# Output projection by token blocks instead of by column halves, with two token blocks routed early and the other two apart

## The chip, the cores and the metric

The kernel runs on one core of a Trainium2 chip. The metric is the device time of one launch in microseconds; the median of three runs is given. The engines are named as the profile names them: PE is TensorE (matmuls; PEld its weight loads), DVE is VectorE, ACT is ScalarE, POOL is GpSimd, SP issues the DMA transfers.

## The reference, cut to what matters

One encoder layer over 512 tokens of 1024 channels: three mixers, merged by gates, one output projection, layer norm, then a mixture of 16 experts in which each expert picks its 64 tokens by router affinity, and a second layer norm. The change lies between the merged mixers and the first expert:

```python
x = layer_norm(DN_ALPHA * x + merged @ w_out[l], ln_mix_g[l], ln_mix_b[l])
...
aff = jax.nn.softmax(jnp.einsum('bsd,de->bse', x, router_w).astype(jnp.float32), axis=-1)
gate, idx = lax.top_k(jnp.swapaxes(aff, 1, 2), cap)
xs = jax.vmap(lambda xb, ib: xb[ib])(x, idx)
h = jax.nn.silu(jnp.einsum('becd,edf->becf', xs, w_gate)) * jnp.einsum('becd,edf->becf', xs, w_up)
y = jnp.einsum('becf,efd->becd', h, w_down) * gate[..., None].astype(x.dtype)
```

## The kernel before

The order of instructions on each engine is the order of the code (a manual schedule); engines run ahead of each other until a tile isn't ready. Tokens lie in four blocks of 128 (tb 0 to 3), the 1024 output columns of the projection in two halves of 512.

**Projection.** Each fp32 product is made of three fp32r matmuls (`wo_mm`, L805 to L807): high part of the merged activations (mh) by high weights (woh), mh by low weights (wol), low activations (ml) by woh. The weights arrive raw (wor) and are split into woh and wol by ScalarE and VectorE (`split`, L88 and L89), one slice of 128 rows (k) at a time. Half 0 runs with k outside and the four blocks inside (L1017 to L1023), into four PSUM banks pw0 to pw3; half 1 runs block by block (`pass2`), with the routing of earlier blocks between its pieces.

**Routing.** `resid` (L931, L932) adds the projection to alpha times x (in the tile xres) and takes statistics of the row half. `route_t` (L954) transposes a block's half to channels first on TensorE, ScalarE copies it to x1T (L955, in the tile hbt). `route_m` (L962) multiplies by the router weights gW (tile Sg) into the bank prt: four fp32 matmuls, the tokens as the stationary operand, 16 moving columns. As layer norm isn't applied yet, the logits are put right afterwards: `aggr` and `stats` give mean and inverse deviation of a row (rss; L936, L942, L502 to L509), `centered` (L981) subtracts the mean's share, `soft` and `soft2` are the softmax (L988 to L996; the exponential on ScalarE, L991), `route_a` (L1002, L1004) transposes the affinities to affT, 16 experts on partitions. `top64` searches the 64 largest of a stretch of tokens, eight at a time (L1011, L1013): sA over tokens 0 to 255 (blocks 0 and 1), sB over tokens 256 to 511. Behind sB come a threshold, ranks, one-hot matrices (L1146), then `gather` (L1163) and the experts. `rows` (L976, L977) scales the tokens on ScalarE for the gather.

**Weights of the experts.** Each 2 MB quarter of a gate, up or down matrix (e0g, e0u, e0d, e1g, ...) goes to one of ten buffers, which it shares with woh, wol, mh and ml of the projection; SP issues the transfers in program order (L79), and one that waits for its buffer holds those behind it. e0g takes buffers free early; two quarters of e0u follow when woh and wol of half 0 are done with; the other two and two of e0d when woh, wol of half 1 and mh, ml are; the first quarter of e1g when the first quarter of e0g has been multiplied (`ff_mm`, L1215).

Of the kernel before, what the change touches and what calls it, by code (L numbers as in the profile page):

```python
# [10 lines left out]
OP = mybir.AluOpType  # L11
# [17 lines left out]
def tile_hybrid_layer(ctx, tc, pk, w2p, xT, x, wlv, wa, wak, wmb, wout, eg, eu, ed, gb, out):  # L29
    nc = tc.nc  # L30
    V, A, G, PE, SP = nc.vector, nc.scalar, nc.gpsimd, nc.tensor, nc.sync
# [37 lines left out]
    def P(name):  # L69
        return psum.tile([128, 512], F32, name=name, tag="ps")  # L70
# [4 lines left out]
    def C(name, shape, dt=F32):  # L75
        return cpool.tile(shape, dt, name=name)
# [51 lines left out]
    ident = C("ident", [128, 128])  # L128
# [158 lines left out]
    st = {}  # L287
# [211 lines left out]
    def rsqrt(r, h, t):  # L499


        return [lambda: V.tensor_scalar(t.bitcast(I32), h.bitcast(I32), 1, None, op0=OP.logical_shift_right),  # L502
                lambda: V.tensor_scalar(r.bitcast(I32), t.bitcast(I32), -1.0,
                                        float(0x5f3759df - 2 ** 22 - 2 ** 31), op0=OP.mult, op1=OP.add),
                lambda: V.tensor_mul(t, r, r), lambda: V.tensor_mul(t, t, h),
                lambda: V.scalar_tensor_tensor(r, t, -1.5, r, op0=OP.add, op1=OP.mult),
                lambda: V.tensor_mul(t, r, r), lambda: V.tensor_mul(t, t, h),
                lambda: V.scalar_tensor_tensor(t, t, -5.0 / 3.0, t, op0=OP.add, op1=OP.mult),
                lambda: V.scalar_tensor_tensor(r, t, 1.25, r, op0=OP.add, op1=OP.mult)]  # L509

    def weave(a, b):

        for i in range(max(len(a), len(b))):
            run(a[i:i + 1] + b[i:i + 1])

    def run(fs):
        for f in fs:
            f()
# [207 lines left out]
    for n, nm in enumerate(names):  # L726
# [4 lines left out]
        for g in range(nseg[n]):  # L731
            k0, k1 = (8 * g + nseg[n] - 1) // nseg[n], (8 * g + 8 + nseg[n] - 1) // nseg[n]
# [44 lines left out]
    def xr_(tb):  # L777
        return xres[tb // 2][:, tb % 2, :]
# [16 lines left out]
    def wo_split(half, k):  # L795
        c = k // 4
        if (half, 0) not in woh:
            wo_tiles(half)
        return split(wraw[half, c][:, k % 4, :], woh[half, c][:, k % 4, :], wol[half, c][:, k % 4, :])

    def wo_mm(p, half, k, tb):
        c, kk = k // 4, k % 4
        a = mh[c][:, kk, tb * 128:(tb + 1) * 128]
        b = ml[c][:, kk, tb * 128:(tb + 1) * 128]
        PE.matmul(p, a, woh[half, c][:, kk, :], start=k == 0, stop=False)  # L805
        PE.matmul(p, a, wol[half, c][:, kk, :], start=False, stop=False)
        PE.matmul(p, b, woh[half, c][:, kk, :], start=False, stop=k == 7)  # L807
# [37 lines left out]
    for u in range(24):  # L845
        b, j = order[u // 8], u % 8
# [45 lines left out]
    def X(name, shape, dt=F32):  # L892
        return xp.tile(shape, dt, name=name)
# [3 lines left out]
    x1T = hbt.rearrange("p (a b c) -> p a b c", a=4, b=4)  # L897
    xga = X("xga", [128, 1024])
# [9 lines left out]
    rb, gW = (sgf[:, 128 * i:128 * i + 128].rearrange("p (k e) -> p k e", k=8) for i in range(2))  # L908
# [6 lines left out]
    mvs = small[:, 0:8].rearrange("p (a b) -> p a b", a=4)  # L915
    rss, nrs, nmr, rts, mnl, zs = (small[:, 8 + 4 * i:12 + 4 * i] for i in range(6))
# [12 lines left out]
    def resid(tb, half, p):  # L929
        r = xr_(tb)[:, half * 512:(half + 1) * 512]  # L930
        V.scalar_tensor_tensor(r, r, ALPHA, p, op0=OP.mult, op1=OP.add)  # L931
        V.bn_stats(stat[:, tb, half, :], r)  # L932

    def aggr(tb, n):

        return [lambda i=i: V.bn_aggr(mvs[:, i, :], stat[:, i]) for i in range(tb, tb + n)]  # L936

    def stats(tb, n):

        c = slice(tb, tb + n)  # L940
        v = mvs[:, c, 1]
        ops = [lambda: V.tensor_scalar(v, v, H225, H225 * 1e-5, op0=OP.mult, op1=OP.add)]  # L942
        return ops + rsqrt(rss[:, c], v, rts[:, c])

    def every2(d):

        c = d // 2 * 256 + d % 2
        return slice(c, c + 255, 2)

    def route_t(tb, half):  # L950

        p = P("px")
        for k in range(4):
            PE.transpose(p[:, k * 128:(k + 1) * 128], xr_(tb)[:, every2(half * 4 + k)], ident)  # L954
        A.copy(x1T[:, tb], p.rearrange("p (a b) -> p a b", a=4))  # L955

    def route_m(tb, half):

        if not half:
            prt[tb] = P("prt")  # L960
        for k in range(4):
            PE.matmul(prt[tb][:, 0:16], x1T[:, tb, k, :], gW[:, 4 * half + k, :], start=half == k == 0,  # L962
                      stop=half == 1 and k == 3)

    prt = {}
# [6 lines left out]

    def rows(tb):

        r = xr_(tb)
        G.tensor_mul(nmr[:, tb:tb + 1], mvs[:, tb, 0:1], nrs[:, tb:tb + 1])  # L976
        A.activation(r, r, AF.Identity, scale=rss[:, tb:tb + 1], bias=nmr[:, tb:tb + 1])  # L977

    def centered(tb, n):

        return [lambda i=i: V.scalar_tensor_tensor(aff[:, i, :], sW, mvs[:, i, 0:1], prt[i][:, 0:16], op0=OP.mult,  # L981
                                                   op1=OP.subtract) for i in range(tb, tb + n)]

    def soft(tb, n):

        for i in range(tb, tb + n):
            lg = aff[:, i, :]
            V.scalar_tensor_tensor(lg, lg, rss[:, i:i + 1], bW, op0=OP.mult, op1=OP.subtract)  # L988
        V.tensor_reduce(mnl[:, tb:tb + n], aff[:, tb:tb + n, :], axis=AX.X, op=OP.min)
        for i in range(tb, tb + n):  # L990
            A.activation(aff[:, i, :], aff[:, i, :], AF.Exp, scale=-1.0, bias=mnl[:, i:i + 1],  # L991
                         accum_out=zs[:, i:i + 1])

    def soft2(tb, n):
        V.reciprocal(zs[:, tb:tb + n], zs[:, tb:tb + n])
        V.tensor_mul(aff[:, tb:tb + n, :], aff[:, tb:tb + n, :],  # L996
                     zs[:, tb:tb + n, None].to_broadcast([128, n, 16]))

    def route_a(tb, n, beside=()):
        p = P("pat")  # L1000
        for i in range(n):
            PE.transpose(p[:16, i * 128:(i + 1) * 128], aff[:, tb + i, :], ident)  # L1002
        run(beside)
        V.tensor_copy(affT[:, tb * 128:(tb + n) * 128], p[:16, :n * 128])  # L1004
# [8 lines left out]
                ops.append(lambda t=t: V.match_replace(src, t, src, -1.0))  # L1013
        return ops

    pw = [P(f"pw{tb}") for tb in range(4)]
    for k in range(8):  # L1017
        if k + 2 < 8:
            wo_split(0, k + 2)
        if k >= 2:  # L1020
            wo_split(1, k - 2)
        for tb in range(4):
            wo_mm(pw[tb], 0, k, tb)  # L1023
    wo_split(1, 6)
    wo_split(1, 7)

# [1 line left out]
    load_halves(3, [S("e0d30", [128, 2048]), spare.tile([128, 2048], F32, name="e0d31")])  # L1028
    load_pairs(NPAIR)

    pw2 = {}

    def pass2(tb, k0=0, k1=8):
        if k0 == 0:
            pw2[tb] = P("pw2")
        for k in range(k0, k1):
            wo_mm(pw2[tb], 1, k, tb)

    L, R = slice(0, 512), slice(512, 1024)
    G.tensor_mul(gW, pkt[:, PK_RW:PK_RW + 128].rearrange("p (a b) -> p a b", a=8),  # L1040
                 pkt[:, PK_G1:PK_G1 + 8, None].to_broadcast([128, 8, 16]))
    G.tensor_mul(rb, pkt[:, PK_RW:PK_RW + 128].rearrange("p (a b) -> p a b", a=8),
                 pkt[:, PK_B1:PK_B1 + 8, None].to_broadcast([128, 8, 16]))
    A.activation(zs[:, 0:1], one[:, 0:1], AF.Exp)
    for tb in range(4):
        resid(tb, 0, pw[tb])
    for i, t in enumerate((rb, gW)):
        V.tensor_reduce(rsum[:, i, :], t.rearrange("p k e -> p e k"), axis=AX.X, op=OP.add)
    pass2(0)
    pbw = P("pbw")  # L1050
    PE.matmul(pbw[:, 0:32], ones, rsum.rearrange("p a b -> p (a b)"), start=True, stop=True)
    V.tensor_copy(bsW, pbw[:, 0:32].rearrange("p (a b) -> p a b", a=2))
    for tb in range(4):
        route_t(tb, 0)
    resid(0, 1, pw2[0])
    pass2(1, 0, 4)
    for tb in range(2):
        route_m(tb, 0)
        pass2(1, 4 + 2 * tb, 6 + 2 * tb)
    route_t(0, 1)  # L1060
    resid(1, 1, pw2[1])
    pass2(2, 0, 2)
    route_t(1, 1)
    route_m(0, 1)
    pass2(2, 2, 4)
    route_m(1, 1)
    run(aggr(0, 2) + stats(0, 2) + centered(0, 2))
    soft(0, 2)
    soft2(0, 2)
    pass2(3, 0, 3)  # L1070
    route_a(0, 2)
    pass2(3, 3, 4)
    pass2(2, 4, 8)
    sA = top64(topA, affT[:, 0:256])
    run(sA[:6])
    resid(2, 1, pw2[2])
    pass2(3, 4, 8)
    route_m(2, 0)
    route_t(2, 1)
    route_m(3, 0)  # L1080
    run(sA[6:9])
    resid(3, 1, pw2[3])
    route_t(3, 1)
    route_m(2, 1)
    route_m(3, 1)
    run(aggr(2, 2))
    s23 = stats(2, 2)
    weave(s23[:8], sA[9:12])
    weave(s23[8:], centered(2, 2))
    soft(2, 2)  # L1090
    run(sA[12:13])
    soft2(2, 2)
    route_a(2, 2, sA[13:])
    G.tensor_scalar(nrs, rss, -1.0, None, op0=OP.mult)
    for tb in range(4):
        rows(tb)

    def bcast(i, half, dg, scale=1.0, E=V, after=None):

# [34 lines left out]
    for tb in range(4):  # L1134
        PE.matmul(rk[:, :, 1, :], onesb, mk[:, tb:tb + 1, 0, :].to_broadcast([128, 4, 16]), start=False,
                  stop=tb == 3)
# [53 lines left out]
    def acc_(tb):  # L1190
        return acc[tb // 2][:, tb % 2, :]
# [260 lines left out]
    for h, c in enumerate((L, R)):  # L1452
        A.activation(acc_(3)[:, c], pf[3, h], AF.Copy, scale=rss[:, 3:4])
        for tb in range(3):
            r = acc_(tb)[:, c]
# [71 lines left out]
```

## Time and profile before

| | |
|---|---|
| median of 3 runs | 1437.47 us (1436.44 to 1439.5) |
| the profiled execution | 1437.92 us |
| its span, first to last instruction | 1436.2 us |
| PE busy | 1358.9 us (95%) |
| DVE busy | 419.3 us (29%) |
| ACT busy | 292.0 us (20%) |
| HBM read | 446.10 MB |

The span and the device time of the profiled execution differ by 1.7 us, which lie outside of the span. PE's busy share is high in all stages, as the ends of pipelined matmuls are modelled; it doesn't tell whether a stage waits for weights. That is read from the DMA share by stretches and from what SP's queue waits for. Times within the trace count from the first instruction.

### The profile page before, as it was taken

The page shows a single profiled execution, that of the slowest core. Times are in us where ns is not written, and L with a number is a line of the kernel's source. Part 1 is how long each engine was busy: PE and PEld are TensorE (multiplying, and loading weights), DVE is VectorE, ACT ScalarE, POOL GpSimd, SP SyncE. Part 2 cuts the span into 40 slices and gives each one's busy share as a digit, 9 for nine tenths or more (in the row PEclk, how much of TensorE's full clock was granted, in tenths as well). Part 3 has the DMA queues.
Part 4 walks back from the last instruction along what each step waited for, and adds up shares of the span by engine and source line. Part 5 has one row for each costly group of instructions (what it writes and reads, how often), then busy time and mean ns, then how long its engine had stood idle before and what let it go on. Part 6 is the DMA issues. An engine that isn't in the chain of part 4 may idle for free.

```text
span 1436.2 us, 17310 instructions
## 1 busy us (share of the span) xinstructions
PE 1358.9 (95%) x7425; PEld 768.3 (53%) x7425; DVE 419.3 (29%) x878; ACT 292.0 (20%) x554; POOL 24.2 (2%) x49
## 2 busy tenths in 40 slices
PE   9999999999999899999999999988989898898996
PEld 8877777888888753443443443433333343333433
DVE  5593975323445613112011011002001011100315
ACT  4644544222233210110110110110000110011110
POOL 0010000000000000000000000000000000000000
PEclk9999999999999999999999999999999999999998
DMA  6120122223239789999999999999999999999994
GB/s 231 45 90 30 61 75 72 88 93 105 89 126 406 297 327 410 429 427 428 428 426 429 427 428 428 426 428 429 426 427 429 427 429 428 428 428 428 426 403 160
DMA packets 45452, 449.31 MB, mean 313 GB/s; under 512 B 4312, under 2 KB 8536, under 8 KB 19520
## 3 DMA queue, kind: packets, MB, share of 16 engines
q1 hardware_dynamic: 45376, 448.22, 75.6%
q8 instruction: 58, 0.95, 0.3%
q14 instruction: 18, 0.15, 0.0%
HBM read 446.10 MB, written 2.10 MB: 312 GB/s over the span
## 4 chain that ended last, share of the span: by engine, by line
PE 55%; DMA 39%; DVE 3%; SPq 1%; ACT 1%; issue 0%; DVEq 0%; POOL 0%; ACTq 0%
PE py L1224 6%; PE pgt L1215 6%; PE pup L1215 5%; PE pa L266 3%; PE pm L866 3%; PE pm L867 3%; PE pm L868 3%; DMA e13d<-in_ed_dram 3%; DMA e9d<-in_ed_dram 3%; DMA e6u<-in_eu_dram 3%; DMA e10u<-in_eu_dram 3%; PE pa L268 3%; PE pa L267 3%; DMA e12u<-in_eu_dram 3%; DMA e8u<-in_eu_dram 3%; DMA e14u<-in_eu_dram 3%
## 5 line engine op out<-in xcount | busy, mean ns | idle before, releaser
L1208 DVE TENSOR_TENSOR acc<-acc,pcb 128x512 f32<-128x512 f32 x64 | 41.1, 683 | 215.5 <-PE pcb L1206 215.5
L1383 DVE TENSOR_TENSOR hbt<-pup,hbt 128x512 f32<-128x512 f32 (+1 forms) x34 | 22.3, 660 | 279.7 <-PE pup L1215 279.6
L1163 PEld LDWEIGHTS pxg<-Sg,xres 128*128 128x128 f32 x512 | 65.2, 196 | 51.5 <-issue 46.8
L266 PE MATMUL pa<-xh,wb 128*128 128x512 f32 x200 | 82.8, 414 | 0.0
L1163 PE MATMUL pxg<-Sg,xres 128*128 128x128 f32 x512 | 76.2, 292 | 6.5 <-DVE Sg L1146 6.5
L268 PE MATMUL pa<-xh,wb 128*128 128x512 f32 x200 | 78.3, 391 | 0.0
L267 PE MATMUL pa<-xl,wb 128*128 128x512 f32 x200 | 78.2, 391 | 0.0
L866 PE MATMUL pm<-xh,wm 128*128 128x512 f32 x192 | 74.8, 390 | 0.0
L867 PE MATMUL pm<-xl,wm 128*128 128x512 f32 x192 | 74.7, 389 | 0.0
L868 PE MATMUL pm<-xh,wm 128*128 128x512 f32 x192 | 74.7, 389 | 0.0
L1233 DVE SCALAR_TENSOR_TENSOR yl<-py,small,late 64x512 fp32r<-64x512 f32 x30 | 22.5, 750 | 140.9 <-ACT late L1232 140.9
L1232 ACT ACTIVATE late<-py,small 64x512 fp32r<-64x512 f32 x30 | 20.5, 683 | 195.2 <-PE py L1224 183.1
L1165 ACT ACTIVATE xgb<-pxg,pk 128x128 f32<-128x128 f32 x32 | 14.7, 458 | 157.0 <-PE pxg L1163 157.0
L1397 ACT COPY hbt<-pht 128x512 f32<-128x512 f32 (+1 forms) x18 | 9.8, 551 | 168.9 <-PE pht L1396 168.4
L1165 ACT ACTIVATE xga<-pxg,pk 128x128 f32<-128x128 f32 x32 | 14.7, 458 | 142.5 <-PE pxg L1163 142.5
L266 PEld LDWEIGHTS pa<-xh,wb 128*128 128x128 f32 x200 | 37.5, 187 | 11.2 <-issue 2.9
L226 DVE TENSOR_TENSOR wm<-wr,wm 128x1536 fp32r<-128x1536 f32 x24 | 42.0, 1752 | 4.1 <-ACT wm L223 4.1
L1372 ACT ACTIVATE hbt<-pgt 128x512 f32<-128x512 f32 x32 | 19.0, 597 | 116.7 <-PE pgt L1215 116.7
L268 PEld LDWEIGHTS pa<-xh,wb 128*128 128x128 f32 x200 | 37.5, 188 | 8.4
L267 PEld LDWEIGHTS pa<-xl,wb 128*128 128x128 f32 x200 | 37.6, 188 | 6.5
L866 PEld LDWEIGHTS pm<-xh,wm 128*128 128x128 f32 x192 | 36.0, 188 | 7.7 <-issue 0.2
L867 PEld LDWEIGHTS pm<-xl,wm 128*128 128x128 f32 x192 | 36.0, 188 | 7.5
(418 smaller groups left out, 2266.9 us busy)
## 6 DMA issues: line engine op xcount, KB each, us to landing
wr<-in_wmb_dram SPq DMA_DIRECT2D x24, 768.0 KB, 4.3
wr<-in_wa_dram SPq DMA_DIRECT2D x12, 1024.0 KB, 4.8
e0g<-in_eg_dram SPq DMA_DIRECT2D x4, 2048.0 KB, 14.9
e0u<-in_eu_dram SPq DMA_DIRECT2D x4, 2048.0 KB
e1g<-in_eg_dram SPq DMA_DIRECT2D x4, 2048.0 KB, 8.8
e1u<-in_eu_dram SPq DMA_DIRECT2D x4, 2048.0 KB, 15.9
e1d<-in_ed_dram SPq DMA_DIRECT2D x4, 2048.0 KB, 16.0
e2g<-in_eg_dram SPq DMA_DIRECT2D x4, 2048.0 KB, 12.0
```

The source lines that it names most:

```text
L226: sp2[u] = V.tensor_sub(l, raw2[u], f32(h))
L266: PE.matmul(p, w[:, 0, k, :], XH(k), start=k == 0, stop=False)
L267: PE.matmul(p, w[:, 0, k, :], XL(k), start=False, stop=False)
L268: PE.matmul(p, w[:, 1, k, :], XH(k), start=False, stop=k == 7)
L866: PE.matmul(p, h[:, k, :], XH(k), start=k == 0, stop=False)
L867: PE.matmul(p, h[:, k, :], XL(k), start=False, stop=False)
L868: PE.matmul(p, l[:, k, :], XH(k), start=False, stop=k == 7)
L1163: PE.matmul(p[:, 0:128], xr_(tb)[:, every2(d)], Sg[:, tb].rearrange("p a b -> p (a b)"), start=tb == 0, stop=tb == 3)
L1165: A.activation(XG[i % 2][:, d, :], p[:, 0:128], AF.Identity, scale=pkt[:, PK_G1 + d:PK_G1 + d + 1], bias=pkt[:, PK_B1 + d:PK_B1 + d + 1])
L1208: V.tensor_add(r, r, p)
L1215: PE.matmul(p[c][g * 64:(g + 1) * 64, :], l, w[:, g * 1024 + c * 512:g * 1024 + c * 512 + 512], start=k == 0, stop=k == 7)
L1224: PE.matmul(p[g * 64:(g + 1) * 64, :], hT[:, k % 4 * 2 + r, half * 64:(half + 1) * 64], w[:, r * 1024 + dh * 512:r * 1024 + dh * 512 + 512 ...
```

## The change

The projection runs by token blocks: half 0 of blocks 0 and 1 with k outside; then all columns of blocks 0 and 1 (half 1 of block 0, half 1 of block 1), then half 0 and half 1 of block 2, half 0 and half 1 of block 3. Blocks 0 and 1 are routed with the roles of the operands swapped (`route_g`): the router weights gW are stationary (16 columns) and x1T moves (128 columns), block 0 to partitions 0 to 15 of one bank, block 1 to partitions 32 to 47, so that the two use different column groups of the array; ScalarE copies the logits to lgT and one transpose brings both back to tokens first (plg). Blocks 2 and 3 keep `route_m`, but each has its own statistics, softmax, transpose to affT and scaling. The search sA is cut into other pieces.

```diff
     def rows(tb):
-        r = xr_(tb)
-        G.tensor_mul(nmr[:, tb:tb + 1], mvs[:, tb, 0:1], nrs[:, tb:tb + 1])
+        r, c = xr_(tb), slice(tb, tb + 1)
+        G.tensor_scalar(nrs[:, c], rss[:, c], -1.0, None, op0=OP.mult)
+        G.tensor_mul(nmr[:, c], mvs[:, tb, 0:1], nrs[:, c])
...
-    pw = [P(f"pw{tb}") for tb in range(4)]
+    pw = {}
+    def wo_pass(tb, half, k0=0, k1=8):
+        if k0 == 0:
+            pw[tb, half] = P("pw")
+        for k in range(k0, k1):
+            wo_mm(pw[tb, half], half, k, tb)
     for k in range(8):
...
-        for tb in range(4):
-            wo_mm(pw[tb], 0, k, tb)
+        for tb in range(2):
+            wo_pass(tb, 0, k, k + 1)
...
+    lgT = xga[0:48, 768:896]
+    def route_g(half):
+        if not half:
+            st["prg"] = P("prg")
+        for k in range(4):
+            for j in range(2):
+                PE.matmul(st["prg"][32 * j:32 * j + 16, 0:128], gW[:, 4 * half + k, :], x1T[:, j, k, :],
+                          start=half == k == 0, stop=half == 1 and k == 3)
+    G.memset(lgT, 0.0)
...
-    for tb in range(4):
-        resid(tb, 0, pw[tb])
+    for tb in range(2):
+        resid(tb, 0, pw[tb, 0])
...
-    pass2(0)
+    wo_pass(0, 1)
...
-    for tb in range(4):
+    for tb in range(2):
         route_t(tb, 0)
-    resid(0, 1, pw2[0])
-    pass2(1, 0, 4)
+    resid(0, 1, pw[0, 1])
+    wo_pass(1, 1, 0, 3)
+    route_g(0)
+    route_t(0, 1)
+    wo_pass(1, 1, 3, 8)
+    resid(1, 1, pw[1, 1])
+    wo_pass(2, 0, 0, 3)
+    route_t(1, 1)
+    run(aggr(0, 2) + stats(0, 2))
+    wo_pass(2, 0, 3, 5)
+    route_g(1)
+    for j in range(2):
+        A.copy(lgT[32 * j:32 * j + 16, :], st["prg"][32 * j:32 * j + 16, 0:128])
+    wo_pass(2, 0, 5, 7)
+    plg = P("plg")
+    PE.transpose(plg[:, 0:48], lgT, ident[:48, :48])
...
+    run(centered(0, 2))
+    soft(0, 2)
+    wo_pass(2, 0, 7, 8)
+    resid(2, 0, pw[2, 0])
+    soft2(0, 2)
+    wo_pass(2, 1, 0, 5)
+    route_a(0, 2)
...
     run(sA[:6])
...
+    wo_pass(2, 1, 5, 8)
+    route_t(2, 0)
     route_m(2, 0)
+    resid(2, 1, pw[2, 1])
+    wo_pass(3, 0, 0, 3)
     route_t(2, 1)
+    run(sA[6:9])
+    wo_pass(3, 0, 3, 6)
+    route_m(2, 1)
+    wo_pass(3, 0, 6, 8)
+    run(sA[9:12])
+    resid(3, 0, pw[3, 0])
+    run(aggr(2, 1))
+    weave(stats(2, 1), sA[12:])
...
+    route_t(3, 0)
+    wo_pass(3, 1, 0, 4)
     route_m(3, 0)
...
+    wo_pass(3, 1, 4, 6)
+    route_a(2, 1)
+    wo_pass(3, 1, 6, 8)
+    resid(3, 1, pw[3, 1])
     route_t(3, 1)
     route_m(3, 1)
...
+    run(aggr(3, 1) + stats(3, 1) + centered(3, 1))
+    soft(3, 1)
+    soft2(3, 1)
+    route_a(3, 1)
+    rows(3)
```

The first place is the loop over k on TensorE, before the change: the first step of k, up to the third block. pw0_3555 to pw3_3558 are the banks of blocks 0 to 3.

```order
L805 MATMUL pw0_3555<-woh0_3476,mh_3141 128x512
L806 MATMUL pw0_3555<-wol0_3477,mh_3141 128x512
L807 MATMUL pw0_3555<-woh0_3476,ml_3142 128x512
L805 MATMUL pw1_3556<-woh0_3476,mh_3141 128x512
L806 MATMUL pw1_3556<-wol0_3477,mh_3141 128x512
L807 MATMUL pw1_3556<-woh0_3476,ml_3142 128x512
L805 MATMUL pw2_3557<-woh0_3476,mh_3141 128x512
L806 MATMUL pw2_3557<-wol0_3477,mh_3141 128x512
L807 MATMUL pw2_3557<-woh0_3476,ml_3142 128x512
```

The same place after the change; pw_3557 and pw_3561 are the banks of blocks 0 and 1.

```order
L805 MATMUL pw_3557<-woh0_3476,mh_3141 128x512
L806 MATMUL pw_3557<-wol0_3477,mh_3141 128x512
L807 MATMUL pw_3557<-woh0_3476,ml_3142 128x512
L805 MATMUL pw_3561<-woh0_3476,mh_3141 128x512
L806 MATMUL pw_3561<-wol0_3477,mh_3141 128x512
L807 MATMUL pw_3561<-woh0_3476,ml_3142 128x512
```

After the sixth matmul the next slice of the weights is asked for now, where two more blocks used the same slice before.

The second place is TensorE at the routing of the first half of block 2 after the change (xres_3491 holds x of blocks 2 and 3; woh_3476 is the weight of half 0).

```order
L805 MATMUL pw<-woh_3575,mh 128x512
L806 MATMUL pw<-wol_3576,mh 128x512
L807 MATMUL pw<-woh_3575,ml 128x512
L954 MATMUL px<-ident,xres_3491 128x128 x4
L962 MATMUL prt<-Sg,hbt 128x16 x4
L805 MATMUL pw<-woh_3476,mh 128x512
```

The router product (L962) reads the copy of the transposes (L954) that stand directly before it. Before the change the product of block 0's first half had stood far behind its transposes; where the two stood side by side, the product was another block's:

```order
L807 MATMUL pw_3819<-woh_3589,ml 128x512
L954 MATMUL px<-ident,xres_3489 128x128 x4
L962 MATMUL prt<-Sg,hbt 128x16 x4
L805 MATMUL pw_3819<-woh_3589,mh 128x512
L806 MATMUL pw_3819<-wol_3590,mh 128x512
```

Here the transposes are block 1's and the product block 0's, whose transposes stand six projection matmuls earlier.

The third place is TensorE behind the last projection matmul, before the change (L1109 begins the broadcasts that follow the routing).

```order
L806 MATMUL pw_3867<-wol_3590,mh 128x512
L807 MATMUL pw_3867<-woh_3589,ml 128x512
L962 MATMUL prt<-Sg,hbt 128x16 x4
L954 MATMUL px<-ident,xres_3491 128x128 x4
L962 MATMUL prt<-Sg,hbt 128x16 x4
L954 MATMUL px<-ident,xres_3491 128x128 x4
L962 MATMUL prt<-Sg,hbt 128x16 x8
L1002 MATMUL pat<-ident,pk 16x128 x2
L1109 MATMUL pbc<-Sg,one 128x128 x16
```

And after it:

```order
L806 MATMUL pw<-wol_3576,mh 128x512
L807 MATMUL pw<-woh_3575,ml 128x512
L954 MATMUL px<-ident,xres_3491 128x128 x4
L962 MATMUL prt<-Sg,hbt 128x16 x4
L1003 MATMUL pat<-ident,pk 16x128
L1141 MATMUL pbc<-Sg,one 128x128 x16
```

Of the 16 router matmuls and 8 transposes behind the projection 4 and 4 are left, those of block 3's second half; the others stand ahead of the last projection matmul.

## Rows read from the trace of the kernel before

**Rows 1.** Stretches: busy us (count) of PE, PEld, DVE, ACT, POOL; clock, DMA share, GB/s.

```profile
482.00:492.00 10.00, 9.89 (x52) 8.10 (x52) 7.41 (x23) 0.70 (x4) 0.00 (x0) 1.00 0.02 7
512.00:516.00 4.00, 4.00 (x23) 1.65 (x19) 0.00 (x0) 0.46 (x1) 0.00 (x0) 1.00 0.08 35
700.00:1300.00 600.00, 552.70 (x2816) 226.97 (x2814) 73.74 (x140) 58.06 (x106) 0.31 (x2) 1.00 1.01 427
```

**Rows 2.** Timeline of SP's transfers: start, us, line, what, count; us spans the count.

```profile
462.01 0.80 SPq L79 DMA_DIRECT2D e0u<-in_eu_dram  x2
491.10 0.80 SPq L79 DMA_DIRECT2D e0u<-in_eu_dram  x2
516.11 0.33 SPq L79 DMA_DIRECT2D e1g<-in_eg_dram  x1
569.65 0.33 SPq L79 DMA_DIRECT2D e1d<-in_ed_dram  x1
```

**Rows 3.** Timeline of PE: start, us, line, operation, form, count.

```profile
440.29 0.39 PE L805 MATMUL pw<-woh,mh 128*128 128x512 f32 x1
443.23 0.39 PE L806 MATMUL pw<-wol,mh 128*128 128x512 f32 x1
...
476.70 0.40 PE L807 MATMUL pw<-woh,ml 128*128 128x512 f32 x1
...
490.90 0.39 PE L807 MATMUL pw<-woh,ml 128*128 128x512 f32 x1
...
491.94 0.70 PE L954 MATMUL px<-ident,xres 128*128 128x128 f32 x4
...
497.87 0.58 PE L1002 MATMUL pat<-ident,pk 128*16 128x128 f32 x2 [2.08 <-DVE pk L996]
```

**Rows 4.** Timeline of DVE, 439 to 520 us.

```profile
443.27 9.02 DVE L89 TENSOR_TENSOR wol<-wor,woh 128x512 fp32r<-128x512 f32 x14
...
477.14 0.69 DVE L931 SCALAR_TENSOR_TENSOR xres<-xres,pw 128x512 f32<-128x512 f32 x1 [7.80 <-PE pw L807]
...
478.47 0.33 DVE L936 BATCH_NORM_AGGREGATE small<-Sg 128x2 f32<-128x12 f32 x2
...
480.70 0.23 DVE L981 SCALAR_TENSOR_TENSOR pk<-Sg,small,prt 128x16 f32<-128x16 f32 x1
...
495.83 0.23 DVE L981 SCALAR_TENSOR_TENSOR pk<-Sg,small,prt 128x16 f32<-128x16 f32 x1
...
498.94 0.42 DVE L1011 MAX8 xga<-xga 16x8 f32<-16x256 f32 x1
```

**Rows 5.** DMA packets from 453 to 455 us, by size.

```profile
DMA packets 119, 0.84 MB, mean 420 GB/s; under 512 B 15, under 2 KB 15, under 8 KB 18
```

**Rows 6.** Chain of work that ended last, 420 to 640 us: start, us, what.

```profile
474.83 0.80 PE prt L962 x8
475.62 0.33 PE pw L805
...
477.10 0.47 PE px L954 x4
```

**Rows 7.** Timeline of PE where 64-wide matmuls stand side by side.

```profile
632.17 0.32 PE L1174 MATMUL pst<-ident,Sg 128*64 128x128 f32 x1
632.18 0.32 PE L1175 MATMUL pst<-ident,Sg 128*64 128x128 f32 x1
632.33 0.27 PE L1174 MATMUL pst<-ident,Sg 128*64 128x128 f32 x1
```

**Rows 8.** Timeline of ACT, 439 to 520 us; in brackets the idle time before.

```profile
492.74 0.59 ACT L955 COPY hbt<-px 128x512 f32<-128x512 f32 x1 [8.67 <-PE px L954]
...
496.92 0.29 ACT L991 ACTIVATE pk<-pk,small 128x16 f32<-128x16 f32 x1
...
497.21 4.62 ACT L977 ACTIVATE xres<-xres,small 128x1024 f32<-128x1024 f32 x4
```

**Rows 9.** A stretch as in the first group, with the granted clock.

```profile
500.00:504.00 4.00, 3.59 (x17) 3.60 (x18) 3.73 (x13) 1.83 (x2) 3.74 (x11) 0.50 1.00 426
```

More of the change, by code (lines that the diff above doesn't have):

```diff
@@ L1029, in tile_hybrid_layer @@
     load_pairs(NPAIR)
[L1031 to L1037, printed above, removed]
-    L, R = slice(0, 512), slice(512, 1024)
+    L, R = slice(0, 512), slice(512, 1024)
+    lgT = xga[0:48, 768:896]
[7 more added lines that the diff above has]
+    G.memset(lgT, 0.0)
     G.tensor_mul(gW, pkt[:, PK_RW:PK_RW + 128].rearrange("p (a b) -> p a b", a=8),
@@ L1052, in tile_hybrid_layer @@
     V.tensor_copy(bsW, pbw[:, 0:32].rearrange("p (a b) -> p a b", a=2))
-    for tb in range(4):
+    for tb in range(2):
         route_t(tb, 0)
-    resid(0, 1, pw2[0])
-    pass2(1, 0, 4)
-    for tb in range(2):
[L1058 to L1073, printed above, removed]
+    resid(0, 1, pw[0, 1])
[14 more added lines that the diff above has]
+    PE.transpose(plg[:, 0:48], lgT, ident[:48, :48])
@@ L1074, in tile_hybrid_layer @@
+    for j in range(2):
+        prt[j] = plg[:, 32 * j:32 * j + 16]
+    run(centered(0, 2))
[5 more added lines that the diff above has]
+    route_a(0, 2)
+    for tb in range(2):
+        rows(tb)
     sA = top64(topA, affT[:, 0:256])
     run(sA[:6])
-    resid(2, 1, pw2[2])
-    pass2(3, 4, 8)
+    wo_pass(2, 1, 5, 8)
+    route_t(2, 0)
     route_m(2, 0)
+    resid(2, 1, pw[2, 1])
+    wo_pass(3, 0, 0, 3)
     route_t(2, 1)
+    run(sA[6:9])
@@ L1080, in tile_hybrid_layer @@
+    wo_pass(3, 0, 3, 6)
[5 more added lines that the diff above has]
+    weave(stats(2, 1), sA[12:])
+    run(centered(2, 1))
+    soft(2, 1)
+    soft2(2, 1)
+    rows(2)
+    route_t(3, 0)
+    wo_pass(3, 1, 0, 4)
     route_m(3, 0)
-    run(sA[6:9])
-    resid(3, 1, pw2[3])
+    wo_pass(3, 1, 4, 6)
+    route_a(2, 1)
+    wo_pass(3, 1, 6, 8)
+    resid(3, 1, pw[3, 1])
     route_t(3, 1)
-    route_m(2, 1)
     route_m(3, 1)
-    run(aggr(2, 2))
@@ L1087, in tile_hybrid_layer @@
[L1087 to L1096, printed above, removed]
+    run(aggr(3, 1) + stats(3, 1) + centered(3, 1))
[3 more added lines that the diff above has]
+    rows(3)
     def bcast(i, half, dg, scale=1.0, E=V, after=None):
```

## The prediction, made before the changed kernel ran

> **What bounds the kernel now.** I first read the stretches of time with the DMA share. The weights of the experts keep the DMA engines full, at 427 GB/s, nearly to the end [rows 1], so what counts is when that steady flow starts. Before it there are two holes: 482 to 492 (7 GB/s) and 512 to 516 (35 GB/s). The queue that issues the transfers (SP) says whom they wait for, by what starts just then. The second pair of expert 0's up weights (e0u) goes out at 491.10, when the last projection matmul (issued at 490.90) is done with woh and wol; the first weights of expert 1 (e1g) go out at 516.11, when TensorE has finished with the first quarter of expert 0's gate weights; and the third part of e1d goes out at 569.65, after TensorE's first gate step of expert 1 [rows 2, 3]. After 569.65 the flow never stops again. So the chain that sets the end runs over TensorE until there: projection, routing, top-64 search, gather, expert 0, the first step of expert 1. A microsecond gained or lost between 440 and 509 comes out at the end whole, as long as the DMA has delivered what is asked.
>
> In that stretch two points matter. E is the end of the last projection matmul: 490.90 plus one step of 0.226 (13 steps from 440.29 to 443.23), so 491.13 [rows 3]. S is the start of the top-64 search of the second half of the tokens on VectorE, 498.94 [rows 4]. Behind S the order of instructions is unchanged: 15 searches, threshold, ranks, one-hot, gather. The forecast is therefore the shift of S.
>
> **The change, part by part.** The 192 projection matmuls stay: 192 x 0.2262 = 43.4 us. From 440.29 to 491.13 that leaves 7.4 us of other TensorE time before E. I build the same sum for the new order.
>
> (a) The loop over k now takes two token blocks, so a step of k lasts 6 matmuls instead of 12. The splits of the weights, which VectorE makes one every 0.64 us (9.02/14) from 443.27 on [rows 4], keep their order. The second matmul of k=2 is the 14th, due at 443.23 [rows 3]; its wol slice is the first of these 14 and is ready about 0.7 later, at 444.0. TensorE waits 0.8, and all that is queued behind it waits too. Later slices arrive ahead: k=3 needs the second by 445.4, k=7 the ninth (449.1) by 450.9. Bound: 0 to 1 us; I take 0.8.
>
> (b) VectorE now reads x (xres) at about 452 instead of 460. Its 4 KB packets have passed by 453: of the 119 packets from 453 to 455 only 18 are small [rows 5], and the first half, which blocks 0 and 1 use, comes ahead of the second. No price; a late x would hold VectorE and then the ones-matmul pbw by as much.
>
> (c) route_m of blocks 0 and 1 goes: four groups of four matmuls at 0.80, and 0.1 each for the slower first matmul behind (0.33 for 0.23) [rows 6], 3.6 us. In comes route_g twice: 8 matmuls with 16 weight columns and 128 moving columns, two blocks side by side in column groups 0 and 32. No such matmul is in the trace. The nearest: two 64-wide fp32 matmuls over 128 columns (L1174, L1175) start 0.01 apart and repeat after 0.16 [rows 7]. Eight such pairs of passes make 1.3; with fewer weight columns 0.9 is the floor I allow. Serial, a full-width transpose step is 0.12 (0.47/4) per pass [rows 6], so 16 passes make 1.9. I take 1.1, as the start times 0.01 apart speak for side by side, and 0.1 for the return: 2.4 for both. The Trainium skill has a rule against this (TensorEngine Tiling (Array Packing), Key Properties): a change of tiling mode drains TensorE. Here the four changes would cost 0.16 each at most, the overlap of a pass of 0.39 with the next at 0.23, 0.6 in place of my 0.2; no run so far shows this for 32-column groups.
>
> (d) plg, one transpose of the logits of two blocks: 0.25 with its return. The two ACT copies ahead of it (at most 0.59 each, the price of one four times as wide [rows 8]) are hidden by six projection matmuls (1.36).
>
> (e) Blocks 2 and 3 are routed apart. Ahead of E now stand: pbw with 8 transposes, 1.2; three groups of transposes at 0.47 [rows 6], 1.4; two route_m at 0.9, 1.8; three pat transposes (0.29 each at a lowered clock [rows 3]), 0.7 with returns. Two new waits: route_m(2,0) stands directly behind its own transposes. ACT starts that copy 0.80 after the first transpose (491.94 to 492.74) and takes 0.59 [rows 3, 8]; so the group lasts 1.45 + 0.9 = 2.35, about 0.9 of it waiting. And route_t(3,0) stands directly behind the last matmul of block 3's first half: residual add 0.44 after that matmul's issue (476.70 to 477.14), 0.72 long [rows 3, 4], so 0.95 of waiting and 0.47 of work. In both the next projection pass is queued behind.
>
> Sum before E: 0.8 + 2.4 + 0.25 + 1.2 + 1.4 + 1.8 + 0.7 + 2.35 + 1.42 = 12.3, against 7.4: E moves by +4.9, to 496.0.
>
> (f) The tail from E to S is 7.81 now. After the change only block 3 is left. With the rows of two blocks: the residual add starts at E+0.21 (0.44 after the last matmul's issue, less its step), the first centring 3.56 later (477.14 to 480.70), the search 3.11 after the last centring (495.83 to 498.94): 6.9. One block saves one aggregate (0.17), one softmax step (0.2, like the centring) and one exponential (0.29) [rows 4, 8]: 6.2. Bounds 6.0 to 6.9. Tail -1.6. TensorE's own part (transposes at E+0.95, route_m to E+3.3) ends before VectorE's statistics do, E+3.6.
>
> Sum: +4.9 - 1.6 = **+3.3 us**.
>
> (g) Moved beside it. ACT's scaling of blocks 0 and 1 (1.2 us each [rows 8]) now comes before its copy for route_m(2,0); by the same walk ACT is free 2.9 us earlier; without that cover up to 2.4. POOL gets three more small instructions, while it is idle. On SP, the first two e0u transfers wait for woh and wol of the first half, now held until block 3's first half is done: about 488.0 instead of 462.01 [rows 2]. Six pairs of 2 MB are then due, 12.6 MB at 427 GB/s, 29.5 us: until 518.1. e1g is asked for at 516.11 + 3.3 = 519.4, so the DMA is ready 1.3 us before; without this cover the lateness would be 1:1.
>
> **The rivals.** (1) The column groups don't run side by side (the change doesn't do what it says): two times 0.8 more, +4.9, 1442.8 on the profiled execution's scale. For it: weights of 16 columns are new here; against it the 0.01 us of [rows 7]. 12%. (2) Only the tail counts: the new order's waits fall into time that TensorE has anyway, E stays, S comes 1.6 earlier, 1436.3. It decides if E comes before 492.7, that is if less than 1.6 of the 4.9 appears. For it: the tail holds one block instead of two. Against it: the 7.4 us of other work before E are just what its groups cost, so TensorE has no spare time there. 10%. (3) The DMA, not TensorE, sets the start of the flow: it is ready at 518.1 whatever TensorE does, against e1g's issue at 516.11 now: +2.0 at most, 1439.9. For it: 29.5 us of transfers behind one release; against it e1g's issue waits for TensorE at 516.11. With half of my waits (0.8 + 0.9 + 0.95) missing S would come to the same, +2.0. 25% for both. (4) The clock. Between 500 and 504 the granted clock is 0.50 of full, the 1.2 GHz level, after TensorE, whose last route_m had ended by the centring at 495.83, had only two pat transposes to do [rows 3, 4, 9]. After the change it is sparsely busy for the 6.2 us from E to S instead of for those last 3.1. If it falls before route_m(3,1), that group and pat can double, +1.1 more: +4.4, 1442.3. 8%. The Trainium skill (TensorE: Matmul & The Clock Gate, PE-mode transpose) holds that transposes don't count as TensorE activity, which would favour this; no row here isolates it.
>
> **How the numbers follow.** The sum is made against the profiled execution, 1437.92 us: 1441.2. The median shown is 0.45 lower, so I forecast 1440.8; the rivals' times likewise come 0.45 lower against it. My own case has 45%, +2.3 to +4.3 by the bounds of (a), (c), (f): 1439.8 to 1441.8. The range reaches from 1437.9 (below it lies rival 2, above it all of 3 but a little) to 1443.4 (rival 1 with a mode drain). A measurement can tell about 0.2%, 2.9 us. Slower than that: two thirds of my own case, rivals 1 and 4 and a few of 3, 53%; within it: the last third of my own case, nearly all of rival 3 and half of rival 2, 42%; faster by more: 5%, the part of rival 2 in which E comes earlier than now, because the four route_m are gone and route_g costs next to nothing.
>
> **What would show it.** After: E near 496 and S near 502.2; a gap on TensorE at 443.2 to 444; one before route_m(2,0) and one before route_t(3,0), 0.9 each; route_g at 1.1 with both blocks' rows in pairs; DMA empty from 472 to 488.5 and hardly afterwards; e1g issued near 519.5. The forecast is wrong if E comes before 494, if e1g's issue isn't followed 1:1 by the end, or if route_g takes 2 us.

## The result and the profile after

The changed kernel takes 1445.0 us (median of 5 runs, 1442.49 to 1446.85) against 1437.47 before; the ratio is 1.0057, 95% interval 1.0044 to 1.0070; the medians lie 7.5 us apart. The forecast was 1440.8, range 1437.9 to 1443.4: the sign was right, the size less than half of what came.

The shares of the page hardly move (PE busy 1361.8 us, 94%), so the stages have to be read. TensorE's timeline after the change, with the idle time and its releaser in brackets:

```profile
438.99 0.39 PE L805 MATMUL pw<-woh,mh 128*128 128x512 f32 x1
...
442.72 0.50 PE L806 MATMUL pw<-wol,mh 128*128 128x512 f32 x1 [0.31 <-DVE wol L89]
...
459.56 1.05 PE L1049 MATMUL prg<-hbt,Sg 128*16 128x128 f32 x16
...
477.84 0.63 PE L954 MATMUL px<-ident,xres 128*128 128x128 f32 x4
479.14 1.06 PE L962 MATMUL prt<-Sg,hbt 128*128 128x16 f32 x8 [0.68 <-ACT hbt L955]
...
488.01 0.75 PE L954 MATMUL px<-ident,xres 128*128 128x128 f32 x4 [0.78 <-DVE xres L931]
...
491.13 0.39 PE L807 MATMUL pw<-woh,ml 128*128 128x512 f32 x1
494.18 1.07 PE L962 MATMUL prt<-Sg,hbt 128*128 128x16 f32 x8 [2.66 <-ACT hbt L955]
...
496.70 0.63 PE L807 MATMUL pw<-woh,ml 128*128 128x512 f32 x1
...
499.40 0.39 PE L807 MATMUL pw<-woh,ml 128*128 128x512 f32 x1
500.57 0.74 PE L954 MATMUL px<-ident,xres 128*128 128x128 f32 x4 [0.78 <-DVE xres L931]
```

The projection begins at 438.99 here and began at 440.29 before [rows 3]; these 1.3 us come from the stages ahead of the change. This kernel and x1, x2 and x3 below have the same code up to there and begin the projection between 438.67 and 440.57, so such a difference comes without a change of code, and I count from there. E, the end of the last projection matmul, is 499.40 + 0.23 = 499.63, 60.6 us after the beginning instead of 50.8. The search of the second half (S) and the transfers that hang on it:

```profile
505.81 0.42 DVE L1012 MAX8 xga<-xga 16x8 f32<-16x256 f32 x1
```

```profile
487.02 0.80 SPq L79 DMA_DIRECT2D e0u<-in_eu_dram  x2
499.60 0.80 SPq L79 DMA_DIRECT2D e0u<-in_eu_dram  x2
...
523.12 0.33 SPq L79 DMA_DIRECT2D e1g<-in_eg_dram  x1
```

The tail from E to S is 6.18 instead of 7.81 us; from the projection's beginning to S ("the stretch" below) it is 66.8 instead of 58.65 us [rows 3, 4], +8.2. From S to e1g's issue it is 17.3 instead of 17.2: the delay of this stage is made before S, the largest single piece of it where TensorE stands 2.66 us before block 3's router product. (The profiled execution ends 8.9 us later than the one before, 1446.85 against 1437.92: it began the projection 1.3 earlier, lost 8.2 up to S, and 1.7 more much later, at expert 4; see what stays open.) The releaser is ScalarE's copy; ScalarE's timeline says why it is late:

```profile
492.13 0.31 ACT L992 ACTIVATE pk<-pk,small 128x16 f32<-128x16 f32 x1 [8.59 <-DVE small L990]
492.35 0.18 ACT L992 ACTIVATION_READ_ACCUMULATOR pk<-pk,small 128x1 f32 x1
492.44 1.22 ACT L978 ACTIVATE xres<-xres,small 128x1024 f32<-128x1024 f32 x1
493.57 0.56 ACT L955 COPY hbt<-px 128x512 f32<-128x512 f32 x1
```

The transposes of block 3's first half were issued from 488.01, but in ScalarE's queue their copy stands behind block 2's exponential (which waits for VectorE's statistics until 492.13, ScalarE idle for 8.59 us) and behind block 2's scaling. Shortly after this gap the granted clock falls to half, the 1.2 GHz level while projection matmuls run (stretches as in [rows 1]; the clock is the third figure from the end):

```profile
491.50:494.00 2.50, 0.02 (x1) 0.00 (x0) 0.86 (x5) 1.87 (x4) 0.40 (x2) 1.00 1.01 433
494.00:496.00 2.00, 1.82 (x12) 1.69 (x13) 0.00 (x0) 0.13 (x1) 0.00 (x0) 0.97 0.98 418
496.00:499.00 3.00, 3.00 (x9) 2.17 (x8) 0.28 (x1) 0.00 (x0) 0.00 (x0) 0.50 0.84 360
```

A projection matmul takes 0.63 us there (496.70 in the first view) instead of 0.39, and they follow each other at 0.43 instead of 0.23.

### The profile page after: what moved, and what is told of

The parts are those of the page before. It is cut to its first block, busy times and chain, and to the rows that moved or that the text cites. A ratio compares the mean times of both kernels' runs of the same rounds, so it can differ in the third digit from the quotient of the medians.

```text
span 1445.0 us, 17326 instructions
## 1 busy us (share of the span) xinstructions
PE 1361.8 (94%) x7426; PEld 766.8 (53%) x7426; DVE 422.4 (29%) x892; ACT 292.6 (20%) x556; POOL 24.5 (2%) x53
## 4 chain that ended last, share of the span: by engine, by line
PE 57%; DMA 37%; DVE 4%; SPq 1%; ACT 1%; issue 1%; DVEq 0%; POOL 0%; ACTq 0%
PE pgt L1247 7%; PE py L1256 6%; PE pup L1247 6%; PE pa L266 3%; PE pm L866 3%; PE pm L868 3%; PE pm L867 3%; DMA e12g<-in_eg_dram 3%; DMA e8g<-in_eg_dram 3%; PE pa L268 3%; PE pa L267 3%; DMA e14u<-in_eu_dram 3%; DMA e10d<-in_ed_dram 3%; DMA e11u<-in_eu_dram 3%; DMA e12d<-in_ed_dram 3%; DMA e10g<-in_eg_dram 3%
## 5 line engine op out<-in xcount | busy, mean ns | idle before, releaser
L1195 PEld LDWEIGHTS pxg<-Sg,xres 128*128 128x128 f32 x512 | 65.2, 196 | 51.4 <-issue 46.8
L868 PEld LDWEIGHTS pm<-xh,wm 128*128 128x128 f32 x192 | 36.0, 188 | 7.6
L866 PEld LDWEIGHTS pm<-xh,wm 128*128 128x128 f32 x192 | 36.0, 188 | 7.5 <-issue 0.2
```

Of the source, the lines that this page charges most:

```text
L866: PE.matmul(p, h[:, k, :], XH(k), start=k == 0, stop=False)
L868: PE.matmul(p, l[:, k, :], XH(k), start=False, stop=k == 7)
L1195: PE.matmul(p[:, 0:128], xr_(tb)[:, every2(d)], Sg[:, tb].rearrange("p a b -> p (a b)"), start=tb == 0, stop=tb == 3)
```

## The experiments

Two readings were open. Theory A: the forecast's sum holds, and what it missed is the copy's place in ScalarE's queue with the clock drop behind it. Theory B: the late loads of expert 0 or the sparser TensorE would have shown anyway. Where a stretch is given, it is read as above from each kernel's own profile, that is from one execution.

**x1: the copy ahead of block 2's softmax.**

```diff
+    route_t(3, 0)
     run(aggr(2, 1))
     weave(stats(2, 1), sA[12:])
     run(centered(2, 1))
     soft(2, 1)
     soft2(2, 1)
     rows(2)
-    route_t(3, 0)
     wo_pass(3, 1, 0, 4)
```

> The transposes of block 3's first half are issued before block 2's softmax in the program, so that their copy stands ahead of block 2's exponential and scaling in ScalarE's queue; TensorE's order is unchanged. Theory A (the part of the slowdown that the forecast missed is TensorE's 2.66 us wait for this copy behind those two, and the low clock from 495.9 to 499.3 that follows it, 1.4 us): the stretch from the first projection matmul to the search of the second half shrinks from 66.8 to about 62.8 us, and the time from 1445.0 to about 1441, which is the forecast. Theory B (the copy's wait is filled by a lack that would show anyway: the DMA, which now loads expert 0 late, or the sparser TensorE, lowers the clock and holds the chain): the stretch stays within 1 us of 66.8, the time at 1444 to 1445.

The stretch is 62.3 us (the forecast's sum had 58.65 + 3.3 = 61.95), the time 1440.21 against 1436.97 of the kernel before, ratio 1.0024 (1.0013 to 1.0034). The projection's first and last matmul and the search:

```profile
438.67 0.39 PE L805 MATMUL pw<-woh,mh 128*128 128x512 f32 x1
...
494.60 0.40 PE L807 MATMUL pw<-woh,ml 128*128 128x512 f32 x1
```

```profile
500.93 0.42 DVE L1012 MAX8 xga<-xga 16x8 f32<-16x256 f32 x1
```

ScalarE copies at once, and TensorE's router product follows its neighbour without a gap:

```profile
488.47 0.59 ACT L955 COPY hbt<-px 128x512 f32<-128x512 f32 x1 [5.25 <-PE px L954]
```

```profile
490.81 0.39 PE L807 MATMUL pw<-woh,ml 128*128 128x512 f32 x1
491.04 0.96 PE L962 MATMUL prt<-Sg,hbt 128*128 128x16 f32 x8
```

This is theory A. Theory B would have kept 66.8.

**x2: only block 2's scaling behind the copy.**

```diff
     soft2(2, 1)
-    rows(2)
     route_t(3, 0)
     wo_pass(3, 1, 0, 4)
+    rows(2)
     route_m(3, 0)
```

> Only the scaling of block 2 (1.2 us on ScalarE) moves behind the copy of block 3's first half; the exponential stays ahead of it. Theory A: the wait of 2.66 us shrinks to about 1.5, the stretch by 1.1 to 65.7; if the shorter gap no longer lowers the clock, by another 1.4 to 64.3. Theory B: no change of the stretch or the time beyond 0.5 us.

The stretch is 64.1 us, the ratio 1.0038 (1.0024 to 1.0052). The gap is 1.54 us as the profile counts it, and the projection runs on at full clock (1.00 from 440 to 500); the clock falls at 501.6 only, behind E (498.53). This is the lower of the two figures expected under A.

```profile
494.63 1.07 PE L962 MATMUL prt<-Sg,hbt 128*128 128x16 f32 x8 [1.54 <-ACT hbt L955]
```

**x3: the gap filled with idle matmuls.**

```diff
     wo_pass(3, 1, 0, 4)
+    keep(10)
     route_m(3, 0)
```

> Ten idle matmul passes' worth of work (10 matmuls of 128 columns into an unused bank, about 2.4 us) fill TensorE's wait before route_m of block 3's first half; nothing else changes, and their product is not used. Theory A with the clock as a part of its own: the wait stays, but the clock stays at full between 495.9 and 499.3, the stretch shrinks by 1.4 us to 65.4, the time to about 1443.6. If the low clock is not due to this gap, the stretch stays at 66.8 or grows a little.

The stretch is 65.2 us, the ratio 1.0034 (1.0021 to 1.0048). The copy is as late as before, but the clock stays up:

```profile
491.43 2.39 PE L971 MATMUL pkeep<-ident,one 128*128 128x128 f32 x20
494.25 1.06 PE L962 MATMUL prt<-Sg,hbt 128*128 128x16 f32 x8 [0.43 <-ACT hbt L955]
```

```profile
493.00:499.00 6.00, 4.87 (x29) 3.71 (x27) 0.95 (x3) 1.20 (x2) 0.00 (x0) 1.00 0.93 396
```

From this router product to E it is 498.13 - 494.25 = 3.9 us here and 499.63 - 494.18 = 5.45 in the changed kernel: the low clock costs 1.6 us there, and it goes when the gap is filled.

**x4: all new waits covered.** Besides x1's move, a third slice of the weights is split ahead, and both groups of transposes stand earlier.

```diff
             wo_split(0, 1)
+            wo_split(0, 2)
...
-        if k + 2 < 8:
-            wo_split(0, k + 2)
+        if k + 3 < 8:
+            wo_split(0, k + 3)
...
-    wo_pass(2, 1, 5, 8)
     route_t(2, 0)
+    wo_pass(2, 1, 5, 8)
     route_m(2, 0)
...
+    wo_pass(3, 1, 0, 2)
+    route_t(3, 0)
     run(aggr(2, 1))
...
     rows(2)
-    route_t(3, 0)
-    wo_pass(3, 1, 0, 4)
+    wo_pass(3, 1, 2, 5)
     route_m(3, 0)
-    wo_pass(3, 1, 4, 6)
+    wo_pass(3, 1, 5, 7)
     route_a(2, 1)
-    wo_pass(3, 1, 6, 8)
+    wo_pass(3, 1, 7, 8)
```

> All the new waits of TensorE are covered: a third weight slice is split ahead of the projection, block 2's first transposes stand three steps of k before its router product, block 3's first transposes two steps behind the end of its first half and their copy ahead of block 2's softmax. Theory A: of the 9.8 us by which the projection ends later 4.0 (copy and clock), 0.8, 0.7 and 0.8 go, the stretch comes to about 60.5 us, still above the 58.7 of the kernel before, because about 3 us of routing work stand ahead of the last projection matmul and only 1.6 come back behind it; time about 1439. Theory B: above 64 us, 1443 or more. A third reading (with the waits gone the new order wins): below 58.7 us and below 1437.

The stretch is 59.3 us, 0.65 above the kernel before; the time 1436.73 against 1436.97, ratio 1.0001 (0.9991 to 1.0011).

```profile
439.42 0.39 PE L805 MATMUL pw<-woh,mh 128*128 128x512 f32 x1
...
492.44 0.40 PE L807 MATMUL pw<-woh,ml 128*128 128x512 f32 x1
```

```profile
498.72 0.42 DVE L1013 MAX8 xga<-xga 16x8 f32<-16x256 f32 x1
```

From the projection's beginning to E it is 2.4 us more than before, the tail is 6.05, 1.76 shorter. The stretch is better than the 60.5 that I expected, and the time sits with the kernel before. What x4 has beyond x1 is worth 3.0 us together; its parts were not run apart. The waits on TensorE that are left lie behind E (waiter and releaser, us in total, times, longest):

```profile
PE pat L1004 <- DVE pk L998: 1.9, 1, 1.9
PE pbc L1143 <- POOL Sg L1139: 1.8, 1, 1.8
PE px L955 <- DVE xres L932: 0.8, 1, 0.8
PE prt L963 <- ACT hbt L956: 0.7, 1, 0.7
```

**x5 and x7: what the swapped product is worth.** x5 is x4 with `route_m` in place of `route_g` for blocks 0 and 1 (and no lgT, no plg). x7 is x4 with the two loops of `route_g` exchanged:

```diff
-        for k in range(4):
-            for j in range(2):
+        for j in range(2):
+            for k in range(4):
```

> The kernel without the waits (x4), but blocks 0 and 1 are routed by route_m as before the change: four groups of 0.80 us with 0.1 behind each come back, the two route_g, the copies to lgT and the transpose plg go. If route_g is worth what its rows show (0.98 for 8 matmuls), the stretch from the first projection matmul to the search grows from 59.3 by 3.6 - 2.2 - 0.3 = 1.1 us to 60.4. If the swapped product gains nothing, it stays at 59.3 or shrinks by the 0.3 of plg.

> The kernel without the waits (x4); the 8 matmuls of route_g are issued block by block, four of block 0 and then four of block 1, instead of in turns, so that neighbours in TensorE's queue use the same column group. If the two groups work side by side in turns, each route_g grows from 0.98 to about 1.9 us and the stretch from 59.3 to 61.1. If the 0.98 come from the narrow weights alone, nothing changes.

x5's stretch is 60.1 (+0.8); x7's is 60.3 (+1.0). Each is read from one profile; their times, 1438.71 and 1435.74, are single runs and tell nothing at this size. The 16 passes of a `route_g` in x4 and in x7, and of two `route_m` in x5 (chain of work):

```profile
459.14 0.98 PE prg L1050 x16
```

```profile
458.42 1.43 PE prg L1050 x16
```

```profile
458.72 1.69 PE prt L963 x16
```

So neither branch of x7's expectation came out whole. Issued in turns, the two column groups save 0.45 per eight matmuls, half of what I had expected of a full overlap; issued block by block, the swapped product still saves 0.26 against `route_m`. x7's +1.0 is twice 0.45 and a little; x5's +0.8 is less than the 1.1 expected, and where the rest went isn't shown.

**x8 and x9: the room in the tail.** TensorE is idle behind E until the residual add of block 3 is there. x8 puts block 3's first router product there, x9 also block 2's affinity transpose.

```diff
-    wo_pass(3, 1, 2, 5)
-    route_m(3, 0)
-    wo_pass(3, 1, 5, 7)
-    route_a(2, 1)
-    wo_pass(3, 1, 7, 8)
+    wo_pass(3, 1, 2, 8)
+    route_m(3, 0)
     resid(3, 1, pw[3, 1])
+    route_a(2, 1)
     route_t(3, 1)
```

(This is x9 against x4; x8 leaves `route_a(2, 1)` ahead of the last step of k.)

> The kernel without the waits (x4), with block 3's first router product moved behind the last projection matmul, where TensorE waits 0.95 us for the residual add. If the reading of the tail is right (VectorE's chain sets it, TensorE has room), the projection ends 0.9 us earlier, the tail stays at 6.05, the stretch comes to about 58.4 us, 0.2 below the kernel before; the time is the same as before within what five rounds can tell (1436 to 1437). If the product delays the transposes behind it, the tail grows by as much and the stretch stays at 59.3.

> As x8 (block 3's first router product behind the last projection matmul), and block 2's affinity transpose behind that product as well, so that no projection matmul is queued behind a wait for VectorE's softmax of block 2. x8 had gained 0.2 us only, since TensorE came to that transpose earlier and waited 0.55 there. If that is the whole reason, the projection ends 0.9 us earlier than in x8 (52.2 after its start), the tail grows by the one copy on VectorE (0.28) to 6.4, the stretch comes to 58.6, that of the kernel before, and the time stays within 0.1% of it. If the wait only moves again, the stretch stays at 59.2.

x8: the stretch is 59.2 us, not 58.4, the ratio 1.0000 (0.9990 to 1.0010). Of the 0.9 us 0.7 were given back at once: TensorE now came to block 2's affinity transpose before VectorE had its softmax ready (issued at 491.29, due at 490.58).

```profile
491.29 0.27 PE L1004 MATMUL pat<-ident,pk 128*16 128x128 f32 x1 [0.55 <-DVE pk L998]
```

x9: the stretch is 58.3 us, the projection 52.2 long as expected, the tail still 6.05 where 6.4 was expected.

```profile
438.88 0.39 PE L805 MATMUL pw<-woh,mh 128*128 128x512 f32 x1
...
490.88 0.39 PE L807 MATMUL pw<-woh,ml 128*128 128x512 f32 x1
```

```profile
497.16 0.42 DVE L1013 MAX8 xga<-xga 16x8 f32<-16x256 f32 x1
```

The time is 1436.37 against 1437.19, ratio 0.9996 (0.9987 to 1.0005): the shortest stretch of all, 0.4 us below the kernel before, and no difference that the times can show.

| kernel | projection to E, us | E to S, us | stretch, us | ratio of times (interval) |
|---|---|---|---|---|
| before | 50.8 | 7.8 | 58.7 | 1 |
| changed | 60.6 | 6.2 | 66.8 | 1.0057 (1.0044 to 1.0070) |
| x2 | 58.0 | 6.2 | 64.1 | 1.0038 (1.0024 to 1.0052) |
| x3 | 59.1 | 6.1 | 65.2 | 1.0034 (1.0021 to 1.0048) |
| x1 | 56.2 | 6.1 | 62.3 | 1.0024 (1.0013 to 1.0034) |
| x4 | 53.3 | 6.1 | 59.3 | 1.0001 (0.9991 to 1.0011) |
| x8 | 53.1 | 6.1 | 59.2 | 1.0000 (0.9990 to 1.0010) |
| x9 | 52.2 | 6.1 | 58.3 | 0.9996 (0.9987 to 1.0005) |

Within the intervals the time follows the stretch: 8.2 us more of it are 0.57% of 1437, the ratio's own figure, though that it agrees to the last digit is luck, since 1.7 us of the profiled execution lie at expert 4; x1's 3.6 would be 0.25%, measured 0.24%; x3's 6.5 would be 0.45%, near the upper edge of its interval.

## Why the prediction was wrong

**The step that failed** is (e), the sum before E: "two route_m at 0.9". For route_m(2,0) I had followed the copy through ScalarE (2.35 us in the sum; 2.3 measured, from 477.84 to the second projection matmul behind at 480.37, less a step of 0.23). For route_m(3,0) I took the price without its copy, and the prediction gives no reason for putting that wait at nothing; twelve projection matmuls stand between its transposes and it. Neither did (g) see it: it checked ScalarE's queue for the scaling of blocks 0 and 1, and not for block 2's exponential and scaling, which the program also puts ahead of a copy that TensorE needs. The copy was 5.5 us behind its transposes (488.01 to 493.57), while the twelve matmuls cover 2.8 (488.51 to 491.36). Of the 4.9 us by which E came later than forecast (+9.8 for +4.9), 2.8 are this wait (491.36, the due time, to 494.18), 1.6 the low clock behind it, as x1 and x3 show, and 0.5 small differences, of which 0.3 can be read: plg took 0.41 for 0.25 (470.82 to 471.68 on TensorE, less two steps), block 3's first transposes with their wait 1.54 for 1.42 (486.83 to 488.82, less two steps). With the copy moved and nothing else, x1 has E at +5.3 and the stretch at +3.6, for +4.9 and +3.3 in the forecast.

**The clock** was rival 4, with 8% and +1.1 us for a fall behind E. That it could fall inside of the projection, behind a wait of the new order's own making, the prediction didn't consider, and there it cost 1.6. It fell behind E as well, at 502.75, in the middle of block 3's last router product (1.31 us for its eight passes, 1.06 in x1 and x4):

```profile
502.05 1.31 PE L962 MATMUL prt<-Sg,hbt 128*128 128x16 f32 x8 [0.73 <-ACT hbt L955]
```

```profile
502.00:512.00 10.00, 6.41 (x31) 6.02 (x32) 8.16 (x33) 1.53 (x3) 5.12 (x15) 0.54 1.00 425
```

There it cost little: the tail is 6.18 us here and in x2, where the product was hit, and 6.05 to 6.12 in the other runs, where it ran at full clock. The Trainium skill (TensorE: Matmul & The Clock Gate, PE-mode transpose) holds that transposes don't count as TensorE activity; no run here isolates that.

**What held.** (a): the second matmul of k=2 stood at 442.72 where 441.94 was due (the 14th from 438.99), 0.8 as forecast. (c): 0.98 us for the eight matmuls, for 1.1, and 1.19 with the way in and out (468.25 to 469.90 from the last projection matmul ahead to the second behind, less two steps of 0.23), for 1.2. Way in and out came to 0.21 per route_g, against 0.1 around a route_m [rows 6] and 0.32 with the prediction's price for two drains. The Trainium skill (TensorEngine Tiling (Array Packing), Key Properties) holds that a change of tiling mode drains TensorE. About half of the 0.2 that this price would have added is seen, and what makes it no run isolates. Rival 1 asked whether the groups work side by side: they do in part (x7). (e), the two waits that I had priced: 0.68 and 0.78 as the profile counts them from the modelled ends, 0.9 and 0.95 from the due times. (f): tail 6.18 for 6.2. (g) and rival 3: e0u went out 25 us later than before, and e1g was still issued at the same distance behind S; in x4, with e0u nearly as late (485.61), the time is that of the kernel before, so the late transfers cost nothing that the times show. The sign "DMA empty from 472 to 488.5 and hardly afterwards" failed in its second half: with E late, the DMA engines stood still again from 499 to 500.5 and from 522 to e1g's issue at 523.12.

Rival 2 (only the tail counts) is refuted: the tail's 1.6 us did come, and E paid six times as much (9.8), three times as much with the copy moved (x1: 5.3). Even in x4, with the waits gone, E moves by 2.4 for a tail 1.8 shorter.

The range's upper end, 1443.4, doesn't follow from its parts: rival 1 comes to 1442.35 on the forecast's scale, and drains of 0.6 in place of 0.2 make it 1442.75. The measured 1445.0 lies above either.

**What stays open.** The profiled execution of the changed kernel has another low stretch at expert 4, 680.2 to 683.6, behind which all later transfers go out another 1.7 us later; x2 and x3 have one as well, the other profiles have none there. Whether it makes part of the spread from run to run (1442.49 to 1446.85) isn't shown, and what starts it was not tried. Open too is the rest of the 0.5 us above. How often the low stretch inside of the projection comes isn't known either, since each kernel has one profiled execution.

## What to carry to other kernels

When work is moved so that TensorE needs a copy by another engine soon, follow that copy through the engine's own queue, with every instruction that the program puts ahead of it and what those wait for; a distance of many matmuls on TensorE is no cover if a 0.3 us exponential that waits for a third engine stands in front. Price a TensorE wait above the wait itself where the matmuls behind it would run at a lower clock: here 2.8 us of waiting, counted from when the product was due, cost 4.5 against x1, and x2's 1.7 us (492.93 to 494.63) only 1.8. A shorter tail is worth only what isn't paid for it ahead (x4: tail 1.8 shorter, E 2.4 later): count TensorE's total work first.

## What the runs showed of the hardware that was not expected

The clock fell about 1.7 us after TensorE had taken up work again (494.18 to 495.9), and stayed low for 3.4 us of dense projection matmuls; a gap of 1.54 us in x2 had no such effect, and none followed where x3 filled the gap with idle matmuls. Each is one execution.

Two fp32 products of 16 stationary columns in different column groups, issued in turns, follow at 0.061 us per pass (0.98/16); in the same group at 0.089 (1.43/16). The 64-wide ones of [rows 7] had suggested starts 0.01 apart and repeats at 0.16 per pair, 0.08 per pass. The turns are worth a factor of 1.46 here, not two; why not more isn't shown.
